# Two-layer hybrid decoder on one core: forms of the w_out product made earlier, one product keyed behind another, the norm's transposes without their key

## The chip, the core and the metric

The kernel runs on one NeuronCore of a Trainium2 chip. TensorE (PE) multiplies, VectorE (DVE) and ScalarE (ACT) do elementwise work and empty the PSUM banks, GpSimd (POOL) computes small powers, SyncE (SP) issues the DMAs. Each engine takes its own instructions in the order in which they stand; engines wait for one another by semaphores. The metric is the device time of one execution in microseconds (us): the median of three runs of the kernel before is 2274.98 us (2274.42 to 2275.09).

## The reference

Two decoder layers on 512 tokens of width 1024, all in fp32. Cut to what matters here:

```python
def hybrid_layer(x, ...):
    proj = rmsnorm(x, norm1_g) @ w_in
    y_ssd, y_mla, y_gdn = ...                 # three branches
    mixed = g_ssd * (y_ssd @ w_ssd_out) + g_mla * (y_mla @ w_mla_out) + g_gdn * (y_gdn @ w_gdn_out)
    h = x + mixed @ w_out
    f = jnp.square(jax.nn.relu(rmsnorm(h, norm2_g) @ w_up)) @ w_down
    return h + f
```

The change touches `mixed @ w_out` in both layers, the norm that follows it, and the end of the first layer's `@ w_down` with the next layer's first norm.

## The kernel before, in words

**Precision.** An fp32 operand is split into a high half (a rounded copy, made by ACT) and a low half (the difference, made by DVE). A product of two such operands is three matmuls: high by high, low by high, high by low (`mm3`, lines 196 to 200). Weights are split tile by tile into `whi` (line 170, ACT) and `wlo` (line 171, DVE); each has four buffers, so a cast for a new tile waits until PE has left the tile four places before it.

**Seven products.** `mixed @ w_out` (and `@ w_down`) is done by `seven` as a 2 x 2 block product with seven multiplications in place of eight. Tokens and the inner dimension are cut into halves on one side, the inner dimension and the columns on the other. On the feature side stand sums and differences of blocks, called forms: a11, a12, s1, s2, s4, s3, a22, named in the order in which w_out multiplies them. So a12 is the second product, s4 the fifth, s3 the sixth and a22 the seventh. One product has four weight tiles (k = 0 to 3) and two halves of rows (t = 0, 1), so 4 x 2 x 3 = 24 matmuls of 512 columns. It accumulates on a pair of PSUM banks: the pair x carries a11, s2, s3 and a22, the pair z carries s1 and s4, a12 has two banks of its own (`sm`). After each product that finishes a block of h, DVE adds the bank into h (line 1219), ACT then squares and sums h for the norm (line 289). a22 goes on accumulating on x after s3, so it can start on a bank only when line 1219 has read it.

**Forms.** In w_out a form has four pieces (d = 0 to 3, one per 128 features): `comb` (line 1299, DVE) makes the sum or difference, `put` writes its high half (line 1294, ACT) and low half (line 1295, DVE). Pieces 0 and 1 need features 0, 1, 4 and 5 of `mixed`, which are final before the last part of the third branch's projection; pieces 2 and 3 need features 6 and 7, which that last part gives. It runs in `mid`, between the first and the second product. The forms a12, s1, s2 and s4 lie in the tiles `xh`, `xl` of the normalized input, which PE reads for the last time in that same part (its gate product).

**Norm.** `norm_half` (lines 297 to 312) norms two blocks of 128 tokens: the two halves' sums of squares are added (line 293, DVE), scaled (276, DVE), raised to the power -1/2 (277, POOL), and h is multiplied by that into a tile `f` (303, DVE). PE then transposes both rows' tiles in 16 transposes (line 308), four to a bank, with three banks; ACT (272, `xh`) and DVE (273, `xl`) empty them with the norm's gain. The norm of the first two token blocks is issued ahead of a22, since their h is final after s4 in w_out.

**What sets the order.** A scheduler orders each engine's instructions from priorities and dependencies; it may place a later product's matmuls between those of an earlier one. `behind(key, ins)` adds an order-only edge: the instruction stands behind the matmul that `place(key, ...)` registered, here (stage, form, k, t). It moves places in the queue and adds no semaphore wait. `tc.high_priority()` raises what is issued in it.

Before, the transposes of the first two banks (`k < 4`) carry the key of a22's first weights on the first half, (a22, 0, 0), so they stand behind three of a22's matmuls. The sixth product has no key. The forms are made when their product is issued (`pre(n)`), all four pieces together.

Of the kernel before, what the change touches and what calls it, by code (L numbers as in the profile page):

```python
# [20 lines left out]
P = 128  # L21
S = 512
T = S // P
D = 1024
# [31 lines left out]
def hybrid_kernel(ctx, tc, a, out, depth=2, taps=None):  # L56
# [139 lines left out]
    def mm3(o, ah, al, bh, bl, start, stop, more=False):  # L196

        pe.matmul(o, ah, bh, start=start, stop=False, skip_group_check=more)  # L198
        pe.matmul(o, ah, bl, start=False, stop=False, skip_group_check=more)  # L199
        return pe.matmul(o, al, bh, start=False, stop=stop, skip_group_check=more)  # L200
# [96 lines left out]
    def norm_half(i, xs, ssq, gcol, pl, hs, ls, tag="xr", bufs=4, given=None, key=None):  # L297

        xr = given or []
        for t in (2 * i, 2 * i + 1)[len(xr) :]:  # L300
            rs = row_scale(ssq[t])
            xr.append(mk(pl, [P, D], F32, tag, bufs))
            dve.tensor_scalar(xr[-1], xs[t], rs, None, ALU.mult)
        for k in range(0, KD, 2):
            ps = sm_bank()
            for j in range(4):
                kk = k + j // 2
                x = pe.transpose(ps[:, j * P : (j + 1) * P], xr[j % 2][:, kk * P : (kk + 1) * P], ident)
                if key and k < 4:
                    behind(key, x)  # L310
            for j in range(2):
                split_gain(hs[k + j][:, HALVES[i]], ls[k + j][:, HALVES[i]], ps[:, j * 256 : (j + 1) * 256], gcol(k + j))
# [71 lines left out]
    for ly in range(depth):  # L384
# [810 lines left out]
        def seven(pl, ops, b, sq=None, before_last=None, fin=None, nf=4, pre=None, mid=None, prep=None, early=False, tag=None):  # L1195
# [29 lines left out]
            def mul(ps, n, w, k, t, start):  # L1225
                ah, al = (o[:, k % 2 * 256 + t * P : k % 2 * 256 + (t + 1) * P] for o in ops[n][k // 2])
                place((tag, n, k, t), mm3(ps[t], ah, al, *w[k], start and k == 0, k == 3, not start))
# [37 lines left out]
        with tc.tile_pool(name="wo", bufs=1, reuse_waits="tile") as wo:  # L1265
# [19 lines left out]
            def mid():  # L1285
# [4 lines left out]
                ops["a22"] = ck_pair()  # L1290

# [17 lines left out]
            def forms(n):  # L1309
# [3 lines left out]
                for d in range(4):  # L1313
                    with tc.high_priority() if d > 1 and n in ("a12", "s1") else nullcontext():
                        form(n, d)
# [20 lines left out]
            def n2(i, pl, *tag):  # L1336
                if not nf:
                    nf.extend(hilo_tags(lp, "x"))
                norm_half(i, hts, ssq, lambda k: col(g_n2 + k), pl, *nf, *tag, key=None if i else ((ly, "o"), "a22", 0, 0))
# [19 lines left out]
        with tc.tile_pool(name="ff", bufs=1, reuse_waits="tile") as fp:  # L1359
# [55 lines left out]
            def ends(qd):  # L1415
# [12 lines left out]
                def before_last():  # L1428
                    for t in range(2):
                        fin(t)  # L1430
                    if not last:
                        norm_half(0, hts, h_ssq, lambda k: params[0][:, 124 + k : 125 + k], fp, *nx, "f", 4, key=((ly, "d"), "a22", 0, 0))
# [51 lines left out]
```

## Time and profile before

| what | value |
|---|---|
| median of three runs | 2274.98 us (2274.42 to 2275.09) |
| the profiled execution | 2274.29 us, its span 2272.5 us |
| PE busy | 2252.4 us, 99% of the span, 11758 matmuls |
| weight loads on PE busy | 1867.6 us, 82% |
| DVE busy | 1649.5 us, 73%, 3315 instructions |
| ACT busy | 1186.1 us, 52%, 2444 instructions |
| POOL busy | 65.0 us, 3%, 84 instructions |
| granted TensorE clock, mean | 0.999 |
| DMA | 244.07 MB, mean 107 GB/s |

Times in a row of the timeline are microseconds from the span's start. A row gives start, duration, engine, line, operation, what is written and read (output, an arrow, inputs, without buffer numbers), and in brackets the engine's idle time before it with what ended it. Matmuls overlap: a 512-column matmul has a duration of 0.39 us, but the next starts about 0.23 us after it, so the pitch of the starts says how fast PE goes, and a start that comes later than the pitch is a hole. The ends of PE's instructions are modelled.

### The profile page before, as it was taken

To read this page: it belongs to the slowest core of one execution; us is meant where nothing else is said; L and a number is where in the kernel's file an instruction comes from. 1 tells how busy PE (TensorE), PEld (TensorE's weight loads), DVE (VectorE), ACT (ScalarE), POOL (GpSimd) and SP (SyncE) were. 2 spreads that over 40 slices of the span, in tenths; PEclk is the share of its full clock that TensorE was granted. 3 is DMA by queue.
4 is the path that set the end of the run, shared out by engine and by line. 5 is a ranking of instruction groups with operands and counts; after the bars stand their busy time and mean duration, and the time that the engine had idled before them with its cause. 6 is when DMAs were issued, how large, how long until landed. Compare 5 with 4: busy or idle time off the path is not lost.

```text
span 2272.5 us, 32127 instructions
## 1 busy us (share of the span) xinstructions
PE 2252.4 (99%) x11758; PEld 1867.6 (82%) x11758; DVE 1649.5 (73%) x3315; ACT 1186.1 (52%) x2444; POOL 65.0 (3%) x84
## 2 busy tenths in 40 slices
PE   9999999999999999999999999999999999999998
PEld 8888888888888888888888878888888887888886
DVE  7886567776766778767868865678657667778668
ACT  6666744333443555554656667443344435645545
POOL 1000000000000000000010000000001000000000
PEclk9999999999999999999999999999999999999999
DMA  4223633442225143233132246335422251433231
GB/s 143 81 75 110 190 108 119 137 134 75 84 65 176 56 149 111 93 110 103 52 99 81 71 121 195 104 110 148 121 84 75 66 189 34 167 112 102 84 111 47
DMA packets 220030, 244.07 MB, mean 107 GB/s; under 512 B 34256, under 2 KB 172384, under 8 KB 219872
## 3 DMA queue, kind: packets, MB, share of 16 engines
q1 hardware_dynamic: 219872, 242.02, 34.7%
q8 instruction: 92, 1.51, 0.3%
q14 instruction: 66, 0.54, 0.1%
HBM read 225.53 MB, written 11.74 MB: 104 GB/s over the span
## 4 chain that ended last, share of the span: by engine, by line
PE 95%; DVE 3%; DMA 1%; ACT 1%; issue 0%; POOL 0%; SPq 0%; DVEq 0%; POOLq 0%; ACTq 0%
PE acc L198 24%; PE acc L200 24%; PE acc L199 24%; PE sm L200 3%; PE sm L199 3%; PE sm L198 3%; PE sm L687 1%; PE sm L791 1%; DVE wlo L171 1%; PE yt L703 1%; PE sm L1073 1%; PE sm L802 1%; PE sm L1099 1%; PE yt L200 1%; PE yt L199 1%; PE yt L198 1%
## 5 line engine op out<-in xcount | busy, mean ns | idle before, releaser
L171 DVE TENSOR_TENSOR wlo<-wraw,whi 128x512 fp32r<-128x512 f32 (+1 forms) x536 | 365.4, 686 | 336.3 <-ACT whi L170 325.3
L170 ACT CAST whi<-wraw 128x512 fp32r<-128x512 f32 (+1 forms) x536 | 329.5, 618 | 524.1 <-PE acc L199 339.7
L198 PE MATMUL acc<-xh,whi 128*128 128x512 f32 (+1 forms) x1344 | 525.3, 391 | 0.0
L200 PE MATMUL acc<-xh,wlo 128*128 128x512 f32 (+1 forms) x1344 | 520.4, 388 | 0.0
L199 PE MATMUL acc<-xl,whi 128*128 128x512 f32 (+1 forms) x1344 | 519.2, 387 | 0.0
L200 PEld LDWEIGHTS acc<-xh,wlo 128*128 128x128 f32 x1344 | 252.5, 188 | 49.3
L198 PEld LDWEIGHTS acc<-xh,whi 128*128 128x128 f32 x1344 | 252.5, 188 | 48.4 <-ACT xh L272 0.4
L199 PEld LDWEIGHTS acc<-xl,whi 128*128 128x128 f32 x1344 | 252.7, 188 | 47.6 <-DVE xl L273 0.7
L170 ACT CAST whi<-wr 128x512 fp32r<-128x512 f32 x168 | 104.3, 621 | 107.9 <-PE acc L199 47.7
L198 PE MATMUL acc<-yh,whi 128*128 128x512 f32 x384 | 152.1, 400 | 0.0
L199 PE MATMUL acc<-yl,whi 128*128 128x512 f32 x384 | 150.3, 391 | 0.0
L200 PE MATMUL acc<-yh,wlo 128*128 128x512 f32 x384 | 149.8, 390 | 0.0
L171 DVE TENSOR_TENSOR wlo<-wr,whi 128x512 fp32r<-128x512 f32 x168 | 113.1, 685 | 35.6 <-ACT whi L170 34.7
L728 DVE SCALAR_TENSOR_TENSOR ckl<-acc,pc,ckl 128x511 f32<-128x511 f32 (+2 forms) x168 | 121.2, 743 | 19.2 <-ACT ckl L724 10.9
L198 PEld LDWEIGHTS acc<-yh,whi 128*128 128x128 f32 x384 | 71.5, 188 | 16.4 <-ACT yh L272 2.2
L200 PEld LDWEIGHTS acc<-yh,wlo 128*128 128x128 f32 x384 | 72.1, 188 | 15.1
L199 PEld LDWEIGHTS acc<-yl,whi 128*128 128x128 f32 x384 | 72.1, 188 | 14.2
L198 PE MATMUL acc<-whi,xh 128*128 128x512 f32 (+1 forms) x208 | 80.3, 386 | 1.2 <-DVE ckl L728 1.2
L199 PE MATMUL acc<-wlo,xh 128*128 128x512 f32 (+1 forms) x208 | 79.3, 381 | 0.0
L200 PE MATMUL acc<-whi,xl 128*128 128x512 f32 (+1 forms) x208 | 79.2, 382 | 0.0
L1219 DVE TENSOR_TENSOR h<-h,acc 128x512 f32<-128x512 f32 x120 | 76.9, 679 | 1.3 <-PE acc L200 1.3
L487 ACT ACTIVATE eE<-eE,cum 128x128 f32<-128x128 f32 x192 | 62.5, 390 | 27.9 <-DMA eE<-d_c 26.2
(468 smaller groups left out, 4497.8 us busy)
## 6 DMA issues: line engine op xcount, KB each, us to landing
wraw<-in_w_in_dram SPq DMA_DIRECT2D x144, 512.0 KB, 3.6
wraw<-in_w_up_dram SPq DMA_DIRECT2D x64, 512.0 KB, 3.5
wr<-in_w_down_dram SPq DMA_DIRECT2D x32, 1024.0 KB, 5.1
eE<-d_c SPq DMA_DIRECT2D x48, 256.0 KB, 4.1
wraw<-in_w_mla_out_dram SPq DMA_DIRECT2D x16, 512.0 KB, 3.4
eE<-d_e SPq DMA_DIRECT2D x32, 256.0 KB, 2.9
wraw<-in_w_ssd_out_dram SPq DMA_DIRECT2D x16, 512.0 KB, 3.3
wraw<-in_w_gdn_out_dram SPq DMA_DIRECT2D x16, 512.0 KB, 3.5
```

The source lines that it names most:

```text
L170: act.copy(hi, raw)
L171: dve.tensor_tensor(lo, raw, f32(hi), ALU.subtract)
L198: pe.matmul(o, ah, bh, start=start, stop=False, skip_group_check=more)
L199: pe.matmul(o, ah, bl, start=False, stop=False, skip_group_check=more)
L200: return pe.matmul(o, al, bh, start=False, stop=stop, skip_group_check=more)
L487: act.activation(o[:, i], o[:, i], AF.Relu, scale=-1.0, bias=cum[:, t, h0 + i : h0 + i + 1])
L687: pe.transpose(ps[:, n : n + P], pn[t][:, kb * P : (kb + 1) * P], ident)
L703: pe.matmul(o, v_h, th[:, c : c + w], start=kb == 0, stop=False)
L728: dve.scalar_tensor_tensor(acc[:, d:], ps[:, : S - d], taps_[3 - d], acc[:, d:], ALU.mult, ALU.add)
L791: x = pe.matmul(py[64 * i : 64 * i + 64, c * P : (c + 1) * P], xd[:, t, h * 64 : (h + 1) * 64], e2[h // 4][:, h % 4, :], start=True, stop= ...
L802: pe.matmul(po[:, c * P : (c + 1) * P], st[:, c * P : (c + 1) * P], ctl[:, tok], start=True, stop=True)
L1219: dve.tensor_tensor(hs_, hs_, ps[t], op)
```

## The change

1. In `mid`, behind the last part of the projection, pieces 0 and 1 of a12, s1, s2, s4 and a22 are made at once, in place of with their products; `forms` then makes pieces 2 and 3 only (a11 keeps all four).
2. `mm3` takes a key for its first matmul. In w_out, and in the stage of w_down that is followed by a layer, s3's first matmul on either half stands behind the last of s4.
3. The norm's transposes lose their key. In its place the row scales and the scaling into `f` of the first two token blocks are issued at high priority.

No matmul, transpose, DMA or elementwise operation is added or taken away: each engine has as many rows as before. SP's and POOL's orders don't change. Line numbers move (199 to 201, 200 to 202, 303 to 306, 308 to 311, 1219 to 1220).

```diff
-    def mm3(o, ah, al, bh, bl, start, stop, more=False):
+    def mm3(o, ah, al, bh, bl, start, stop, more=False, key=None):
 
-        pe.matmul(o, ah, bh, start=start, stop=False, skip_group_check=more)
+        x = pe.matmul(o, ah, bh, start=start, stop=False, skip_group_check=more)
+        if key:
+            behind(key, x)
...
         for t in (2 * i, 2 * i + 1)[len(xr) :]:
-            rs = row_scale(ssq[t])
-            xr.append(mk(pl, [P, D], F32, tag, bufs))
-            dve.tensor_scalar(xr[-1], xs[t], rs, None, ALU.mult)
+            with tc.high_priority() if first else nullcontext():
+                rs = row_scale(ssq[t])
+                xr.append(mk(pl, [P, D], F32, tag, bufs))
+                dve.tensor_scalar(xr[-1], xs[t], rs, None, ALU.mult)
...
-                x = pe.transpose(ps[:, j * P : (j + 1) * P], xr[j % 2][:, kk * P : (kk + 1) * P], ident)
-                if key and k < 4:
-                    behind(key, x)
+                pe.transpose(ps[:, j * P : (j + 1) * P], xr[j % 2][:, kk * P : (kk + 1) * P], ident)
...
-                place((tag, n, k, t), mm3(ps[t], ah, al, *w[k], start and k == 0, k == 3, not start))
+                key = (tag, "s4", 3, 1) if tag and early and n == "s3" and k == 0 else None
+                place((tag, n, k, t), mm3(ps[t], ah, al, *w[k], start and k == 0, k == 3, not start, key))
...
                 ops["a22"] = ck_pair()
+                for d in range(2):
+                    for n in ("a12", "s1", "s2", "s4", "a22"):
+                        form(n, d)
...
-                for d in range(4):
+                for d in range(0 if n == "a11" else 2, 4):
```

The two callers of `norm_half`, in `n2` and at the end of w_down, pass `first=not i` and `first=True` in place of the key.

**Order of PE, fifth and sixth product in the first layer's w_out.** acc_1589 and acc_1590 are the pair z, acc_1587 and acc_1588 the pair x; whi_1692 to whi_1698 are s4's weights, whi_1702 is s3's first; xh6 and xh7 hold s4's form. Before:

```order
L200 MATMUL acc_1590_7455<-whi_1692_7884,xl6_1645_7688 128x512
L198 MATMUL acc_1587_7452<-whi_1702_7931,s3h0_1583_7448 128x512
L198 MATMUL acc_1588_7453<-whi_1702_7931,s3h0_1583_7448 128x512
L198 MATMUL acc_1589_7454<-whi_1694_7894,xh6_1637_7680 128x512
L199 MATMUL acc_1589_7454<-wlo_1695_7895,xh6_1637_7680 128x512
```

Of the change:

```order
L202 MATMUL acc_1590_7455<-whi_1692_7888,xl6_1645_7688 128x512
L198 MATMUL acc_1589_7454<-whi_1694_7898,xh6_1637_7680 128x512
L201 MATMUL acc_1589_7454<-wlo_1695_7899,xh6_1637_7680 128x512
...
L202 MATMUL acc_1590_7455<-whi_1698_7918,xl7_1646_7689 128x512
L198 MATMUL acc_1587_7452<-whi_1702_7935,s3h0_1583_7448 128x512
```

s3's first two matmuls stood between s4's first and second weights; now they stand behind all of s4.

**Order of PE, s3, a22 and the transposes there.** f_1729 and f_1731 are the scaled rows of token blocks 0 and 1, ct_0 is the identity, whi_1736 and whi_1738 are a22's first and second weights. Before:

```order
L200 MATMUL acc_1588_7453<-whi_1708_7961,s3l1_1586_7451 128x512
L198 MATMUL acc_1587_7452<-whi_1736_8049,ckh0_1647_7690 128x512
L199 MATMUL acc_1587_7452<-wlo_1737_8050,ckh0_1647_7690 128x512
L200 MATMUL acc_1587_7452<-whi_1736_8049,ckl0_1649_7692 128x512
L308 MATMUL sm_1732_8005<-ct_0_75,f_1729_7997 128x128
L308 MATMUL sm_1732_8005<-ct_0_75,f_1731_8003 128x128
...
L198 MATMUL acc_1587_7452<-whi_1738_8053,ckh0_1647_7690 128x512
```

Of the change:

```order
L202 MATMUL acc_1588_7453<-whi_1708_7965,s3l1_1586_7451 128x512
L311 MATMUL sm_1732_8009<-ct_0_75,f_1729_8001 128x128
L311 MATMUL sm_1732_8009<-ct_0_75,f_1731_8007 128x128
...
L198 MATMUL acc_1587_7452<-whi_1736_8049,ckh0_1647_7690 128x512
L201 MATMUL acc_1587_7452<-wlo_1737_8050,ckh0_1647_7690 128x512
L202 MATMUL acc_1587_7452<-whi_1736_8049,ckl0_1649_7692 128x512
L198 MATMUL acc_1587_7452<-whi_1738_8053,ckh0_1647_7690 128x512
```

Twelve transposes (three banks) change places with a22's first three matmuls. The last four stay behind ten matmuls of a22. At the end of w_down the twelve move in the same way, and the last four move three matmuls back.

**Order of DVE, the norm's scaling in w_out.** h_1573 is h, wlo_1705 to wlo_1709 are low halves of s3's weights, wlo_1737 to wlo_1741 of a22's, nrs_1728 and nrs_1730 the row scales. Before:

```order
L1219 TENSOR_TENSOR h_1573_7426<-h_1573_7426,acc_1590_7455 128x512
L171 TENSOR_TENSOR wlo_1709_7962<-wr01_1575_7433,whi_1708_7961 128x512
L293 TENSOR_TENSOR nrs_1728_7993<-nss_1517_7123 128x1
L171 TENSOR_TENSOR wlo_1737_8050<-wr00_1663_7750,whi_1736_8049 128x512
...
L303 TENSOR_SCALAR f_1729_7997<-h_1573_7426,nrs_1728_7993 128x1024
L171 TENSOR_TENSOR wlo_1739_8054<-wr00_1663_7750,whi_1738_8053 128x512
L303 TENSOR_SCALAR f_1731_8003<-h_1573_7426,nrs_1730_7999 128x1024
L1219 TENSOR_TENSOR h_1573_7426<-h_1573_7426,acc_1587_7452 128x512
```

Of the change:

```order
L1220 TENSOR_TENSOR h_1573_7426<-h_1573_7426,acc_1590_7455 128x512
L171 TENSOR_TENSOR wlo_1709_7966<-wr01_1575_7433,whi_1708_7965 128x512
L295 TENSOR_TENSOR nrs_1728_7997<-nss_1517_7123 128x1
...
L306 TENSOR_SCALAR f_1729_8001<-h_1573_7426,nrs_1728_7997 128x1024
L171 TENSOR_TENSOR wlo_1737_8050<-wr00_1669_7778,whi_1736_8049 128x512
L171 TENSOR_TENSOR wlo_1739_8054<-wr00_1669_7778,whi_1738_8053 128x512
L306 TENSOR_SCALAR f_1731_8007<-h_1573_7426,nrs_1730_8003 128x1024
L171 TENSOR_TENSOR wlo_1741_8058<-wr00_1669_7778,whi_1740_8057 128x512
L1220 TENSOR_TENSOR h_1573_7426<-h_1573_7426,acc_1587_7452 128x512
```

The four small operations on nrs stand together and the first scaling directly behind them; a22's first low half moves behind it, and a third low half of a22 now stands ahead of the eviction of s3.

On ACT the same stage changes in two ways: the two squares that the scaling needs stand together ahead of a22's first cast (before, that cast stood between them), and one of the norm's gain copies (line 272) stands ahead of the two squares of s3's block, the rest behind them.

More of the change, by code (lines that the diff above doesn't have):

```diff
@@ L295, in row_scale, with norm_half @@
         return rs
-    def norm_half(i, xs, ssq, gcol, pl, hs, ls, tag="xr", bufs=4, given=None, key=None):
+    def norm_half(i, xs, ssq, gcol, pl, hs, ls, tag="xr", bufs=4, given=None, first=False):
         xr = given or []
         for t in (2 * i, 2 * i + 1)[len(xr) :]:
-            rs = row_scale(ssq[t])
-            xr.append(mk(pl, [P, D], F32, tag, bufs))
-            dve.tensor_scalar(xr[-1], xs[t], rs, None, ALU.mult)
+            with tc.high_priority() if first else nullcontext():
+                rs = row_scale(ssq[t])
+                xr.append(mk(pl, [P, D], F32, tag, bufs))
+                dve.tensor_scalar(xr[-1], xs[t], rs, None, ALU.mult)
         for k in range(0, KD, 2):
@@ L1338, in n2 @@
                     nf.extend(hilo_tags(lp, "x"))
-                norm_half(i, hts, ssq, lambda k: col(g_n2 + k), pl, *nf, *tag, key=None if i else ((ly, "o"), "a22", 0, 0))
+                norm_half(i, hts, ssq, lambda k: col(g_n2 + k), pl, *nf, *tag, first=not i)
             seven(wo, ops, b, ssq, lambda: n2(0, wo, "f", 2), nf=2, pre=forms, mid=mid, early=True, tag=(ly, "o"))
@@ L1431, in before_last @@
                     if not last:
-                        norm_half(0, hts, h_ssq, lambda k: params[0][:, 124 + k : 125 + k], fp, *nx, "f", 4, key=((ly, "d"), "a22", 0, 0))
+                        norm_half(0, hts, h_ssq, lambda k: params[0][:, 124 + k : 125 + k], fp, *nx, "f", 4, first=True)
                 return dict(sq=h_ssq, before_last=before_last, fin=fin, prep=prep, early=not last, tag=(ly, "d"))
```

## The prediction

> **What bounds the kernel now.** I read the page first, then who TensorE waits for, then the timeline of the stages that the edits touch.
>
> ```profile
> span 2272.5 us, 32127 instructions
> PE 2252.4 (99%) x11758; PEld 1867.6 (82%) x11758; DVE 1649.5 (73%) x3315; ACT 1186.1 (52%) x2444; POOL 65.0 (3%) x84
> ```
>
> TensorE (PE) is idle for 2272.5 - 2252.4 = 20.1 us of the whole span. The change adds or removes no matmul, so it can only win PE's waits at its three places: the two w_out products (one in each layer) and the end of the first layer's w_down. The waits by releaser, in total us, times, longest:
>
> ```profile
> PE acc L198 <- DVE h L1219: 3.5, 3, 1.2
> PE acc L198 <- ACT whi L170: 1.5, 2, 0.8
> ```
>
> Three waits for an eviction of h and two for a weight's high half are the two longest groups. Where they lie, on PE, in time (start, us, in brackets the idle time and its releaser):
>
> ```profile
> 774.29 0.39 PE L198 MATMUL acc<-whi,xh 128*128 128x512 f32 x1
> ...
> 786.53 0.40 PE L200 MATMUL acc<-whi,xl 128*128 128x512 f32 x1
> 787.69 0.73 PE L198 MATMUL acc<-whi,s3h 128*128 128x512 f32 x2 [0.76 <-ACT whi L170]
> ...
> 797.20 0.39 PE L200 MATMUL acc<-whi,s3l 128*128 128x512 f32 x1
> 798.77 0.47 PE L198 MATMUL acc<-whi,ckh 128*128 128x512 f32 x1 [1.18 <-DVE h L1219]
> ...
> 799.53 1.47 PE L308 MATMUL sm<-ct,f 128*128 128x128 f32 x12
> 800.76 0.48 PE L198 MATMUL acc<-whi,ckh 128*128 128x512 f32 x1
> ...
> 802.24 0.39 PE L198 MATMUL acc<-whi,ckh 128*128 128x512 f32 x1
> 802.58 0.63 PE L308 MATMUL sm<-ct,f 128*128 128x128 f32 x4
> ```
>
> This is layer 0: products s1, s2, s4, s3 from 774.29 to 797.20, then a22 with the norm's transposes in it. The second layer has the same two holes, so I count everything of this place twice:
>
> ```profile
> 1914.34 0.74 PE L198 MATMUL acc<-whi,s3h 128*128 128x512 f32 x2 [0.76 <-ACT whi L170]
> 1925.41 0.47 PE L198 MATMUL acc<-whi,ckh 128*128 128x512 f32 x1 [1.18 <-DVE h L1219]
> ```
>
> The pitch of one 512-column matmul comes from the product before, which has no hole:
>
> ```profile
> 769.76 0.39 PE L199 MATMUL sm<-wlo,xh 128*128 128x512 f32 x1
> ...
> 774.07 0.39 PE L200 MATMUL sm<-whi,xl 128*128 128x512 f32 x1
> ```
>
> 19 steps in 4.31 us, 0.2268 us each.
>
> **The sixth product behind the fifth, forms made ahead (term A, w_out only).** s1, s2, s4 and s3 are 4 x 24 = 96 matmuls. Without a hole, first start to last start is 95 x 0.2268 = 21.54 us; the rows say 797.20 - 774.29 = 22.91. So 1.37 us is lost, most of it ahead of 787.69. The cause on ScalarE (ACT):
>
> ```profile
> 787.02 0.62 ACT L170 CAST whi<-wr 128x512 fp32r<-128x512 f32 x1 [0.77 <-PE acc L200]
> 787.74 0.42 ACT L1294 ACTIVATE xh<-fc 128x256 fp32r<-128x256 f32 x1
> ```
>
> PE has s3's first two matmuls in its queue ahead of s4's second weights. Their weight cast can only start when PE has left s4's first weights (same buffer), 0.49 us after the start at 786.53, and the form that s4 needs next (787.74) stands behind that cast on ACT. PE waits for a thing that itself waited for PE. In the new order s4's 24 matmuls stand together, and s4's first two pieces of form were made long before. The key alone would leave PE waiting for that form; both edits are needed. I take all 1.37 off: s3's last matmul starts at 795.83.
>
> What the moved forms cost where they go: for s2 and s4, pieces 0 and 1, four combinations and four low halves on VectorE (DVE), four high halves on ACT.
>
> ```profile
> 753.16 0.69 DVE L171 TENSOR_TENSOR wlo<-wraw,whi 128x512 fp32r<-128x512 f32 x1 [0.50 <-ACT whi L170]
> 755.23 0.76 DVE L1295 SCALAR_TENSOR_TENSOR xl<-fc,xh 128x256 fp32r<-128x256 f32 x2 [1.37 <-ACT xh L1294]
> ...
> 758.60 0.69 DVE L171 TENSOR_TENSOR wlo<-wraw,whi 128x512 fp32r<-128x512 f32 x1 [1.86 <-ACT whi L170]
> ```
>
> Two of them take 0.76, with a pitch of 0.34, so 8 x 0.34 = 2.7 us go into 0.50 + 1.37 + 1.86 = 3.7 us of DVE idleness. On ACT the high halves wait until PE has read the old x tiles, as here, and weight casts queue behind:
>
> ```profile
> 754.77 0.73 ACT L1294 ACTIVATE xh<-fc 128x256 fp32r<-128x256 f32 x2 [1.64 <-PE sm L200]
> ...
> 760.67 0.62 ACT L170 CAST whi<-wr 128x512 fp32r<-128x512 f32 x1 [1.60 <-PE acc L199]
> 763.39 0.62 ACT L170 CAST whi<-wr 128x512 fp32r<-128x512 f32 x1 [2.10 <-PE acc L199]
> ```
>
> A cast comes late by 0.7 us at most, while the four weight buffers hold three more tiles of 2.7 us (763.39 - 760.67) each. So nothing on PE; without this cover it would cost at most 2 x 0.7. The 2.7 us leave the stretch 779.9 to 786.8, where DVE was busy for 6.85 of 6.90 us:
>
> ```profile
> 779.90:786.80 6.90, 6.90 (x30) 5.12 (x29) 6.85 (x15) 3.93 (x8) 0.00 (x0) 1.00 0.00 0
> ```
>
> **Transposes unkeyed, scaling first (term B).** a22 accumulates on the banks that s3 filled, so it must wait until DVE has added them into h. Before, the twelve transposes stood behind a22's first three matmuls and could not fill that wait; now they stand ahead of it. They need both scaled rows f, and the second of these, not s3, now ends last. Rows for the walk:
>
> ```profile
> 792.60 1.28 DVE L1219 TENSOR_TENSOR h<-h,acc 128x512 f32<-128x512 f32 x2
> ...
> 796.01 0.75 DVE L303 TENSOR_SCALAR f<-h,nrs 128x1024 f32<-128x1024 f32 x1 [0.42 <-POOL nrs L277]
> 796.68 0.68 DVE L171 TENSOR_TENSOR wlo<-wr,whi 128x512 fp32r<-128x512 f32 x1
> 797.28 0.75 DVE L303 TENSOR_SCALAR f<-h,nrs 128x1024 f32<-128x1024 f32 x1
> 797.94 1.28 DVE L1219 TENSOR_TENSOR h<-h,acc 128x512 f32<-128x512 f32 x2
> ```
>
> DVE starts its next operation 0.60 us after a wlo or h, 0.67 after an f. The new order on DVE is wlo, wlo, h, h, wlo, four small ones, f, wlo, wlo, f, wlo, h, h. Its second wlo waits for a cast that PE releases after s4's third weights: s4 starts at 774.29 + 48 x 0.2268 = 785.18, those weights' last matmul at 785.18 + 17 x 0.2268 = 789.03; + 0.49 + 0.62 for the cast is 790.14. Then h at 790.75 and 791.35, wlo at 791.95, the first small one at 792.55. From there to the first f the w_down stage, which has this order already, shows 1128.73 - 1127.66 = 1.07 (rows below): f at 793.62, wlo at 794.29 and 794.89, the second f at 795.49, done 796.24. From h's end to PE the rows show 797.94 + 0.68 = 798.62 to 798.77, 0.15 us. So the transposes start at 796.39, 0.33 after s3 (796.06), and take 800.76 - 799.53 = 1.23: 797.62. The first h eviction, behind f and a wlo, is over at 795.49 + 0.67 + 0.60 + 0.68 + 0.15 = 797.59, hidden by them. a22's first three matmuls take 0.76 (798.77 to 799.53), and its second weights start at 798.38. From s3's last matmul to there: 2.55 us, before 800.76 - 797.20 = 3.56. Gain 1.01.
>
> Some goes back. The last four transposes need a bank that DVE frees only after xl1, and between lie ACT's squares of the evicted h:
>
> ```profile
> 798.71 0.63 ACT L289 ACTIVATE fs<-h 128x512 f32<-128x512 f32 x1 [0.46 <-DVE h L1219]
> ...
> 800.17 2.44 ACT L272 ACTIVATE xh<-sm,pc 128x256 fp32r<-128x256 f32 x6
> ```
>
> In the new order ACT has one xh, the two squares, xh2, xh1. The first square follows the first h's end (797.44) by 0.09, the second comes 0.63 later, xh2 0.83 after that (800.17 less the second square's start, 798.71 + 0.63), xh1 0.40 later at 799.39. DVE's xl1 then ends near 800.4 and frees the bank for PE at some 800.55. PE comes there at 798.38 + 1.82 - 0.11 = 800.09 (1.82 is 802.58 - 800.76, 0.11 its own wait: 802.58 - 802.24 less one pitch). That wait is 0.46 where it was 0.11, so 0.35 go back: B = 1.01 - 0.35 = 0.66 at each w_out.
>
> At the w_down end DVE's order stays up to here; only the transposes move on PE.
>
> ```profile
> 1127.66 0.15 DVE L293 TENSOR_TENSOR nrs<-nss 128x1 f32<-128x1 f32 x1
> ...
> 1128.73 0.75 DVE L303 TENSOR_SCALAR f<-h,nrs 128x1024 f32<-128x1024 f32 x1 [0.43 <-POOL nrs L277]
> ...
> 1130.97 0.39 PE L200 MATMUL acc<-whi,mix 128*128 128x512 f32 x1
> ...
> 1131.04 0.74 DVE L303 TENSOR_SCALAR f<-h,nrs 128x1024 f32<-128x1024 f32 x1
> ...
> 1132.52 0.47 PE L198 MATMUL acc<-whi,yh 128*128 128x512 f32 x1 [1.17 <-DVE h L1219]
> ...
> 1134.52 0.48 PE L198 MATMUL acc<-whi,yh 128*128 128x512 f32 x1
> ```
>
> The second f ends at 1131.78; + 0.15 + 1.23 + 0.76 puts a22's second weights at 1133.92, before 1134.52: gain 0.60. The last four transposes now come three matmuls later, so their bank is free.
>
> **Sum.** 2 x (1.37 + 0.66) + 0.60 = 4.66, say 4.6 us. On the profiled execution: 2274.29 (span 2272.5 and 1.79 around it) becomes 2269.7, span 2267.9. The median of the runs is 2274.98, 0.69 above that execution, so I predict 2274.98 - 4.6 = 2270.4 us, 0.20% down. About 0.2%, 4.55 us, is what a measurement of this kernel can tell from no change, so my sum ends on that line.
>
> Bounds: the holes themselves hold 2 x (1.37 + 1.34) + 1.32 = 6.7 us (1.34 is 798.77 - 797.20 less one pitch, 1.32 is 1132.52 - 1130.97 less one); more can hardly come. Below, term B is open, since no row shows the transposes first: between 0 and 1.3 at each place.
>
> **The rivals.**
>
> *The power waits for DVE.* Two powers on POOL take 1.38 us, and the second lies beside the first f. In the new order f, wlo, wlo run back to back. Should the second power get no turn among them, it starts at 795.49, and the second f, with all behind it, is 0.6 later: 4.6 - 2 x 0.6 = 3.4, 2271.6. Against it:
>
> ```profile
> 795.42 1.38 POOL L277 TENSOR_TENSOR nrs<-nrs,nhalf 128x1 f32<-128x1 f32 x2 [101.70 <-DVE nrs L293]
> ```
>
> It ended at 796.80, 0.04 after f's end (796.76) and while the wlo of 796.68 ran; so f may hold it, a wlo hardly. With other small slips of the norm's chain I give it 0.14. (The Trainium skill, SBUF — State Buffer, section "SBUF: two separate sides", says that GpSimd and VectorE share a port pair as an exclusive lock, taken by a DVE operation in a 2-port mode or with two SBUF inputs when GpSimd reads SBUF. By that rule wlo, with two inputs, would hold the power as f does; this row agrees for f and speaks against it for wlo.)
>
> *Everything fits.* The squares and xh interleave better, the bank is free, f is in time: 2 x (1.37 + 1.2) + 0.9 = 6.0, 2269.0. The squares in ACT's order speak against it: 0.16.
>
> *The key only moves the wait.* s4 waits for its last two pieces of form instead, and A is gone: 2 x 0.66 + 0.60 = 1.9, 2273.1. DVE has 2.7 us less in that stretch, so 0.06.
>
> *Slower.* PE takes its queue in order, and with no key the transposes stand ahead of all 24 matmuls of a22. A late second f stops both. To be 4.55 us slower, the three B terms must come to -4.55 - 2.74 = -7.3, that is -2.4 each: from an f that is 3.1 us later than walked, five more DVE operations ahead of it. The order shows none, and DVE has 2.7 us less to do: 0.04.
>
> **How the numbers follow.** The forecast (gain 3.9 to 5.3) has 0.60, and half of it lies beyond 4.55. Faster: 0.31 + 0.16 = 0.47; within: 0.29 + 0.14 + 0.06 = 0.49; slower: 0.04. The range 2268.6 to 2272.4 takes in the first three cases and leaves out s4's wait, the slower case and the tails.
>
> **What would show it.** Right: no wait for whi at the start of s3 in w_out; transposes straight behind s3, with an idle time of some 0.3 us ahead of them; no 1.2 us wait for h; some 0.5 us ahead of the last four transposes; span near 2267.9. Wrong: a wait at s4's third weights (A has moved); transposes more than 1 us behind s3 (the norm's chain); weights late in the gate stage around 750 to 770.

## The result and the profile after

| | before | changed |
|---|---|---|
| median of ten runs | 2274.98 us | 2269.63 us |
| the profiled execution | 2274.29, span 2272.5 | 2269.02, span 2267.2 |
| PE busy | 2252.4 | 2251.3 |

The ratio of the runs is 0.9978 (the two medians alone give 0.9976), with a 95% interval of 0.997 to 0.9986. The interval lies below 1, so the changed kernel is faster. Its upper end is less than the 0.2% away from 1 that the prediction took as its line, so a gain above that line is not shown by the times. Predicted were 2270.4 us and a span of 2267.9. PE's idle time fell from 20.1 to 2267.2 - 2251.3 = 15.9 us. Page and waits of PE in the changed kernel (us in total, times, longest):

```profile
span 2267.2 us, 32128 instructions
...
PE 2251.3 (99%) x11758; PEld 1868.3 (82%) x11758; DVE 1649.1 (73%) x3315; ACT 1185.1 (52%) x2444; POOL 64.6 (3%) x84
```

```profile
PE acc L202 <- DVE wlo L171: 0.6, 1, 0.6
...
PE sm L311 <- DVE f L306: 0.4, 1, 0.4
...
PE sm L311 <- DVE xl L275: 0.2, 1, 0.2
```

The two longest waits of before, for h and whi, are gone from the list. Three small ones are new, and the largest is at a place of which the prediction said nothing. PE's timeline of the first layer's w_out in the changed kernel, with the same steps as shown of before (first matmul of s1, last of s3, transposes, a22's first and second weights, last four transposes, first matmul of w_up):

```profile
773.35 0.39 PE L198 MATMUL acc<-whi,xh 128*128 128x512 f32 x1
...
794.88 0.39 PE L202 MATMUL acc<-whi,s3l 128*128 128x512 f32 x1
795.11 1.57 PE L311 MATMUL sm<-ct,f 128*128 128x128 f32 x12
796.54 0.47 PE L198 MATMUL acc<-whi,ckh 128*128 128x512 f32 x1
...
797.31 0.39 PE L198 MATMUL acc<-whi,ckh 128*128 128x512 f32 x1
...
798.67 0.39 PE L198 MATMUL acc<-whi,ckh 128*128 128x512 f32 x1
799.23 0.63 PE L311 MATMUL sm<-ct,f 128*128 128x128 f32 x4 [0.17 <-DVE xl L275]
...
802.88 0.28 PE L198 MATMUL acc<-xh,whi 128*128 128x256 f32 x1
```

From s1 to s3's last matmul: 794.88 - 773.35 = 21.53 us, no hole. The transposes follow one pitch behind (0.23). From s3's last matmul to a22's second weights it is 2.43 us, where it was 3.56. The last four transposes come 0.56 behind a matmul whose pitch is 0.23. The hole of the gate stage, on PE and on DVE:

```profile
817.63 0.40 PE L201 MATMUL acc<-xl,whi 128*128 128x512 f32 x1
818.66 0.50 PE L202 MATMUL acc<-xh,wlo 128*128 128x512 f32 x1 [0.63 <-DVE wlo L171]
```

```profile
816.78 1.22 DVE L1181 TENSOR_TENSOR wp<-wr,wr 128x1024 f32<-128x1024 f32 x1 [2.18 <-DMA wr<-in_w_down_dram]
817.92 2.49 DVE L171 TENSOR_TENSOR wlo<-wraw,whi 128x512 fp32r<-128x512 f32 x4
```

DVE stood 2.18 us at a sum of w_down weights that waited for its transfer, while the wlo that PE needed stood behind it in DVE's queue. On PE the two starts lie 1.03 us apart where the pitch is 0.23, so 0.80 was lost there (the bracket counts from the modelled end of the matmul before). The casts of those tiles on ACT had begun a microsecond before the sum:

```profile
815.75 2.34 ACT L170 CAST whi<-wraw 128x512 fp32r<-128x512 f32 x4
```

**Stage by stage.** All kernels here issue the same number of matmuls on PE (11758), so the k-th start of one trace can be set against the k-th of another. The table gives what a run won against the profile of before between two marks (762.7 to 807.8 us, 807.8 to 823.2, 1122.8 to 1146.8, 1887.8 to 1933.6 on before's clock; medians of six starts around each mark). These differences are free of what happens elsewhere in the execution: by 762.7 us, ahead of PE's first reordered matmul, the thirteen runs already differ from before by -1.29 to +0.95 us (above 0 is ahead of it). The changed kernel's 0.95 does not come from the moved forms: DVE's order differs only from 743.65 us on, and by 300 us PE was already 0.94 ahead. A wait for `xr` in the first norm, 0.90 us in before (PE at 9.32) and 0.19 in the changed kernel (at 8.85), is 0.71 of it. One run of the kernel changed in the second layer only took 3202.27 us at a granted clock of 0.653; it is in that row's median, which is 2272.46 without it.

| run | first w_out | gate stage behind it | w_down's end | second w_out | time or median, us |
|---|---|---|---|---|---|
| changed | 2.43 | -0.99 | 0.85 | 2.37 | 2269.63 |
| changed, again | 2.43 | -1.06 | 0.84 | 2.34 | 2270.04 |
| forms alone | 1.27 | -0.59 | 0.00 | 1.22 | 2272.22 |
| key alone | -0.59 | -0.70 | 0.00 | -0.67 | 2276.45 (one run) |
| norm's part alone | 0.95 | -0.72 | 0.84 | 0.87 | 2271.55 |
| no key, no priority | 2.43 | -0.97 | 0.82 | 2.35 | 2269.23 (one run) |
| before, again | 0.03 | -0.01 | 0.03 | -0.03 | 2275.30 (one run) |
| sum held | 2.43 | -0.05 | 0.83 | 2.37 | 2268.84 |
| second f first | 2.24 | -0.71 | 0.84 | 2.21 | 2268.60 (one run) |
| last four later | 2.74 | -1.81 | 0.81 | 2.69 | 2270.39 (one run) |
| second layer only | 0.01 | 0.00 | 0.00 | 2.37 | 2272.51 |
| all three | 2.93 | -0.08 | 0.84 | 2.86 | 2268.69 |
| all three, again | 2.92 | -0.07 | 0.87 | 2.86 | 2268.44 |

For the changed kernel the four add up to 2.43 - 0.99 + 0.85 + 2.37 = 4.66 us. That is the prediction's sum to the second digit by luck, since the terms are others: 0.40 and 0.34 more at the two w_out, 0.25 more at w_down's end, and 0.99 lost where nothing was expected. The rest of the 5.27 us between the two profiled executions lies outside the change: 0.95 was there by 762.7 us, and 0.37 went back between w_down's end and the second w_out.

### The profile page after: what moved, and what is told of

Read it like the earlier page. It is cut to its first block, busy times and chain, and to the rows that moved or that the text cites. A ratio compares the mean times of both kernels' runs of the same rounds, so it can differ in the third digit from the quotient of the medians.

```text
span 2267.2 us, 32128 instructions
## 1 busy us (share of the span) xinstructions
PE 2251.3 (99%) x11758; PEld 1868.3 (82%) x11758; DVE 1649.1 (73%) x3315; ACT 1185.1 (52%) x2444; POOL 64.6 (3%) x84
## 4 chain that ended last, share of the span: by engine, by line
PE 95%; DVE 3%; DMA 1%; ACT 1%; POOL 0%; issue 0%; SPq 0%; DVEq 0%; POOLq 0%; ACTq 0%
PE acc L198 24%; PE acc L202 24%; PE acc L201 24%; PE sm L201 3%; PE sm L198 3%; PE sm L202 3%; PE sm L688 1%; PE sm L792 1%; DVE wlo L171 1%; PE yt L704 1%; PE sm L1074 1%; PE sm L1100 1%; PE sm L803 1%; PE yt L201 1%; PE yt L198 1%; PE yt L202 1%
## 5 line engine op out<-in xcount | busy, mean ns | idle before, releaser
L729 DVE SCALAR_TENSOR_TENSOR ckl<-acc,pc,ckl 128x511 f32<-128x511 f32 (+2 forms) x168 | 121.2, 743 | 19.2 <-ACT ckl L725 10.9
```

What stands on the lines that cost most here:

```text
L729: dve.scalar_tensor_tensor(acc[:, d:], ps[:, : S - d], taps_[3 - d], acc[:, d:], ALU.mult, ALU.add)
```

## The experiments

**Forms alone** (key on s3 off; the norm as before):

```diff
-                key = (tag, "s4", 3, 1) if tag and early and n == "s3" and k == 0 else None
+                key = None
```

> Only the early forms; no key on s3, the norm's transposes keyed and its scaling at plain priority, as before. Each engine's order is the same, row for row, as with forms and key together: with its form ready, s4 is taken whole ahead of s3 without the key. Theory (the early forms alone carry term A): from the start of s1 to the start of s3's last matmul 21.5 us in both layers (before 22.91), no whi wait at s3's start, and the norm still behind a22's first weights, so the 1.2 us wait for h stays; total gain near 2 x 1.37 = 2.7 us, profiled execution near 2271.6. In the first layer's gate stage of the feed-forward, the wait for wlo at 818 should be at most 0.3 us, since PE comes there 1.4 us early and not 3.3. Rival (both edits are needed, as the prediction says): 22.9 stays, no gain.

From s1 to s3's last matmul it took 21.53 us in both layers, and the wait for h stayed:

```profile
797.11 0.47 PE L198 MATMUL acc<-whi,ckh 128*128 128x512 f32 x1 [1.27 <-DVE h L1221]
```

The forms carry all of term A without the key. 1.27 and 1.22 us are won at w_out, less than term A's 1.37, since the wait for h grew by 0.1. The time, 2272.22 us, is 0.9991 of before (0.9982 to 1.0). In the gate stage the wait for wlo was 0.27 us, within the 0.3 that was expected, but by the starts on PE the stage lost 0.59.

**Key alone** (no early forms, the norm as before; against the changed kernel, its forms' lines are):

```diff
-                for d in range(2):
-                    for n in ("a12", "s1", "s2", "s4", "a22"):
-                        form(n, d)
...
-                for d in range(0 if n == "a11" else 2, 4):
+                for d in range(4):
```

> Only the key on s3; forms made with their products, norm as before. PE's order in w_out is that of the changed kernel up to the end of s3. Theory (the key only moves the wait): PE waits 1.2 to 1.5 us inside s4 for the second half of its form, s1's start to s3's last matmul stays at 22.5 to 23.1, execution within 0.5 us of 2275. Rival (the key carries term A): 21.5 and a gain of 2.7 us.

From s1's start to s3's last matmul it now took 23.35 and 23.37 us, more than the 22.5 to 23.1 that were expected. PE, inside s4, and ACT there:

```profile
788.61 0.50 PE L198 MATMUL acc<-whi,xh 128*128 128x512 f32 x1 [1.29 <-ACT xh L1297]
```

```profile
787.41 0.62 ACT L170 CAST whi<-wr 128x512 fp32r<-128x512 f32 x1 [0.77 <-PE acc L202]
788.14 0.42 ACT L1297 ACTIVATE xh<-fc 128x256 fp32r<-128x256 f32 x1
```

The key moved the wait from whi to the form, and made it longer: ACT still takes s3's cast ahead of the form, and now PE has nothing in between. 0.59 and 0.67 us were lost at w_out.

**The norm's part alone:** the forms' loops of the diff above taken out, and

```diff
-                key = (tag, "s4", 3, 1) if tag and early and n == "s3" and k == 0 else None
+                key = None
```

> Only the norm's part: transposes without key, scaling at high priority; no early forms, no key on s3. Theory (terms A and B are independent): s1's start to s3's last matmul stays at 22.9, the first transposes start 0.2 to 0.7 us behind s3's last matmul, s3's last to a22's first matmul 1.7 to 2.1, gain 0.6 to 1.0 at each w_out and 0.6 to 0.8 at w_down's end: 1.8 to 2.8 us in all. Rival (the norm is in time only because the early forms took work off DVE): the transposes more than 0.8 us behind s3 and a gain below 1.3 in all.

PE behind s3:

```profile
797.36 0.39 PE L202 MATMUL acc<-whi,s3l 128*128 128x512 f32 x1
797.59 0.27 PE L311 MATMUL sm<-ct,f 128*128 128x128 f32 x1
798.23 1.42 PE L311 MATMUL sm<-ct,f 128*128 128x128 f32 x11 [0.36 <-DVE f L306]
799.40 0.48 PE L198 MATMUL acc<-whi,ckh 128*128 128x512 f32 x1
```

The first transpose needs only the first f and starts at once; the second one waits for the second f. a22 starts 2.04 us behind s3's last matmul. It won 0.95 and 0.87 us at w_out and 0.84 at w_down's end; the time is 0.9988 of before (0.9979 to 0.9998). So each part works without the other: 1.27 + 0.95 = 2.22 against 2.43 together. The 0.2 more together goes with a second f that ends 0.32 us behind s3's last matmul there (below) and 0.81 here (798.17).

**No key, no priority:**

```diff
-            with tc.high_priority() if first else nullcontext():
+            with nullcontext():
...
-                key = (tag, "s4", 3, 1) if tag and early and n == "s3" and k == 0 else None
+                key = None
```

> The changed kernel without the key on s3 and without the high priority of the scaling: early forms and unkeyed transposes only. All five engines have the same order, row for row, as in the changed kernel. Theory (these two edits do nothing): every stage within 0.1 us of the changed kernel's (21.53, 0.23, 1.66, 29.54), time within 1.5 us of 2269.6. Rival (key or priority do something at run time): the whi wait of 0.76 or the h wait of 1.2 is back.

Four stretches of w_out are meant: from s1's first to s3's last matmul, from there to the first transpose and to a22's first matmul, and from s1's first matmul to w_up's. They are 21.53, 0.23, 1.66 and 29.55 us, within 0.03 of the changed kernel in both layers, and each engine has its rows in the changed kernel's order. Two of the four edits do nothing.

**Before, once more.** The forms, the key and the norm's part alone had each lost 0.59 to 0.72 us in the gate stage, even the key, with which PE comes there later than in before. So PE had not simply outrun the transfer. Perhaps the first profile of before was a lucky one:

> The kernel before, unchanged, profiled once more. Its first profile had no wait for wlo in the first layer's gate stage; its w_down weights had landed 9.0 us after the second of their four transfers was issued, against 10.5 to 10.9 us in the five profiles of other kernels so far. Theory (that landing varies by run, and the first profile of before was a lucky one): landing after some 10.5 us and a hole of 0.5 to 0.8 us at that place, execution 274.9 to 275.5 us above 2000. Rival (the hole belongs to the change): landing after 9.0 us and no hole, execution near 2274.3.

DVE there:

```profile
819.12 1.22 DVE L1180 TENSOR_TENSOR wp<-wr,wr 128x1024 f32<-128x1024 f32 x1
820.99 2.50 DVE L171 TENSOR_TENSOR wlo<-wraw,whi 128x512 fp32r<-128x512 f32 x4 [0.66 <-ACT whi L170]
```

There is no wait for the transfer and no hole on PE; the landing took 8.0 us. So the rival holds, as far as one repeat can show it. The execution took 2275.30 us, in the range of the first theory, but 1.29 of that was lost by 762.7 us, ahead of this place.

**The sum held** behind the wlo's of w_up's second column block:

```diff
+                    if c == 1:
+                        lo_c1 = lo_at[0]
+                    held[0] = lo_c1 if qd == 0 and c == 2 else None
                     after(c)
...
-                    dve.tensor_tensor(o[:, q], x[:, q], y[:, q], ALU.add)
+                    x_ = dve.tensor_tensor(o[:, q], x[:, q], y[:, q], ALU.add)
+                    if held[0]:
+                        after_product(x_.ins, held[0].ins)
```

(`lo_at` holds the last wlo that `split_half` issued; `after_product` adds an order-only edge.)

> The changed kernel, with the sum of w_down weight blocks (first quarter of w_down only, in both layers) ordered behind the wlo's of the second column block of w_up; nothing else moves on any engine. Theory (the sum waits for its transfer at the head of DVE's queue and holds back the wlo behind it): DVE makes those wlo from 816.4 on, the wait for wlo at 818 is gone, and 0.8 to 0.9 us are won in the first layer, nothing in the second: about 2268.8. Rival (the wlo are late for another reason, the casts on ACT): the wait stays at 0.6 us and the time at 2269.6.

DVE (line numbers are two higher here):

```profile
817.30 2.50 DVE L173 TENSOR_TENSOR wlo<-wraw,whi 128x512 fp32r<-128x512 f32 x4 [1.79 <-ACT whi L172]
```

The stage lost 0.05 in place of 0.99, though the transfer landed no sooner (10.9 us). So the wait hung on the sum's place in DVE's queue. By times alone this kernel can't be told from the changed one: its ratio to before is 0.9976 (0.9966 to 0.9985).

**The second f first:**

```diff
                     w.append(split_half(raw(k)))
+                    if n == "a22" and f_at[0]:
+                        after_product(lo_at[0].ins, f_at[0].ins)
```

(`f_at` holds the scaling into the second f.)

> The changed kernel, with DVE's second scaled row f ahead of all of a22's wlo (two or three operations later than f now). Prediction's reading (the second f ends last and sets when the transposes end and a22 starts, in w_out and at w_down's end): a22 starts 0.2 us earlier at each w_out (1.46 us behind s3's last matmul in place of 1.66) and 0.4 earlier at w_down's end. Rival (in w_out the eviction of h ends last, at 796.39, and the second f ends last only at w_down's end): twelve transposes in 1.23 us but a22's start at 1.6 to 1.7 in w_out, nothing gained there; 0.3 to 0.4 gained at w_down's end alone.

DVE and PE in the first w_out, and PE at w_down's end:

```profile
792.59 1.58 DVE L308 TENSOR_SCALAR f<-h,nrs 128x1024 f32<-128x1024 f32 x2 [0.38 <-POOL nrs L281]
...
795.89 1.28 DVE L1226 TENSOR_TENSOR h<-h,acc 128x512 f32<-128x512 f32 x2
```

```profile
795.12 1.47 PE L315 MATMUL sm<-ct,f 128*128 128x128 f32 x12
796.72 0.47 PE L200 MATMUL acc<-whi,ckh 128*128 128x512 f32 x1
...
1128.76 1.47 PE L315 MATMUL sm<-ct,f 128*128 128x128 f32 x12
1130.25 0.47 PE L200 MATMUL acc<-whi,yh 128*128 128x512 f32 x1
...
1134.06 0.63 PE L315 MATMUL sm<-ct,f 128*128 128x128 f32 x4
```

In w_out the transposes ran without a gap, and a22 came later, 0.83 us behind the start of h's eviction (795.89 to 796.72), as in the changed kernel (795.71 to 796.54, below). There the eviction ends last, not f. The second f now waited for the second power, so wlo and h moved back by 0.18, and w_out lost 0.19 and 0.16. At w_down's end f was last: a22 came 0.35 earlier. But PE then stood 0.29 us ahead of the last four transposes (0.51 behind a matmul whose pitch is 0.23), and the stage gave 0.84 as before. The gain there was nothing, where 0.3 to 0.4 was expected.

**The last four later:**

```diff
-                pe.transpose(ps[:, j * P : (j + 1) * P], xr[j % 2][:, kk * P : (kk + 1) * P], ident)
+                x = pe.transpose(ps[:, j * P : (j + 1) * P], xr[j % 2][:, kk * P : (kk + 1) * P], ident)
+                if key and k == 6:
+                    behind(key, x)
...
-                norm_half(i, hts, ssq, lambda k: col(g_n2 + k), pl, *nf, *tag, first=not i)
+                norm_half(i, hts, ssq, lambda k: col(g_n2 + k), pl, *nf, *tag, first=not i, key=None if i else ((ly, "o"), "a22", 0, 1))
```

> The changed kernel, with the last four transposes of w_out's norm behind a22's first weights on the second half, five matmuls later. The order also puts both halves of the w_down weight sum ahead of the wlo's at 818, in place of one. Theory: the bank is free when PE gets there, so the 0.33 us ahead of the last four transposes is gone (before them one pitch, 0.23) and a22's end comes 0.3 earlier at each w_out; and the doubled sum makes the wait for wlo in the first layer longer by one sum, 1.1 us, to some 1.8 us. Rival on the first: another bank wait stays ahead of them. Rival on the second (that wait doesn't hang on the sum): it stays at 0.6.

The bank was free: 2.74 and 2.69 us at w_out, 0.3 more than the changed kernel. The gate stage on DVE and PE:

```profile
818.18 2.36 DVE L1183 TENSOR_TENSOR wp<-wr,wr 128x1024 f32<-128x1024 f32 x2 [2.08 <-DMA wr<-in_w_down_dram]
```

```profile
821.20 0.50 PE L202 MATMUL acc<-xh,wlo 128*128 128x512 f32 x1 [1.46 <-DVE wlo L171]
```

Two sums stand ahead of the wlo in place of one, and the loss grew from 0.99 to 1.81. The second sum holds DVE for 2.36 - 1.22 = 1.14 us and cost 0.82.

**The second layer only.** The same lines with `ly` in their conditions, the norm keyed as before where `ly` is 0 and at w_down's end:

```diff
-                for d in range(2):
+                for d in range(2 if ly else 0):
...
-                for d in range(0 if n == "a11" else 2, 4):
+                for d in range(0 if n == "a11" or not ly else 2, 4):
```

> The whole change in the second layer's w_out alone; up to there each engine's order is row for row that of before, the first layer's w_out and w_down end included. Theory one (the slow landing of the w_down weights in the first layer comes with something in the schedule of that layer's w_out): landing 8 to 9 us after the second of the four transfers is issued, as in the two profiles of before, no wait for wlo at 818, and the gain is that of one w_out, 2.4 us. Theory two (it is a property of the whole program, whatever stands near that place): landing after 10.5 to 10.9 us, a wait of 0.3 to 0.6 us there, and a gain of 1.5 to 2.1 us. On the change itself: the second layer's w_out at 21.53, 0.23, 1.66 and 29.55 us, whatever the first layer did.

It won 2.37 us in the second w_out and lost nothing in the first layer's gate stage, where the landing came after 7.94 us. The time is 0.999 of before (0.9981 to 0.9999), 2.40 us less by the medians. Theory two fails. Of theory one it is open what in the schedule would do it.

**All three additions together,** and in w_out a22's second to fourth wlo behind the first eviction of h:

```diff
+                        after_product(lo_at[0].ins, (h_at if mid and k else f_at)[0].ins)
```

(`h_at` holds the first eviction of s3.)

> The changed kernel with the w_down weight sum behind the wlo's of w_up's second column block, the last four transposes of w_out's norm behind a22's first weights on the second half, the second f ahead of a22's wlo (both places), and in w_out a22's second to fourth wlo behind the first eviction of h. Theory (what ends last in w_out is the eviction of h, at w_down's end the second f, then the bank): 0.9 us in the first layer's gate stage, 2 x 0.3 at the last four transposes, 2 x 0.1 to 0.2 at a22's start (1.46 to 1.55 us behind s3's last matmul, now 1.66), 0.35 at w_down's end: 2.1 us below the changed kernel, near 2267.5. Rival (one of them shifts to a wlo that comes late for a22's second or third weights): 0.2 to 0.4 us lost again in each w_out, near 2268.2.

PE behind s3:

```profile
796.59 0.39 PE L204 MATMUL acc<-whi,s3l 128*128 128x512 f32 x1
796.82 1.47 PE L315 MATMUL sm<-ct,f 128*128 128x128 f32 x12
798.04 0.48 PE L200 MATMUL acc<-whi,ckh 128*128 128x512 f32 x1
```

Now the transposes set a22's start (1.46 us behind s3), with no wait up to w_up. It won 2.93 and 2.86 us at the two w_out, lost 0.08 in the gate stage, and won nothing more at w_down's end, where 0.35 was expected. By stages that is 6.55 us against 4.66, 1.9 more than the change. The median, 2268.69 us, is above the 2267.5 that were expected; its ratio to before is 0.9973 (0.9963 to 0.9983).

**The changed kernel and all three again,** on one chip:

> The changed kernel, unchanged, profiled and timed once more beside the kernel with all three additions. So far the w_down weights of the first layer landed 7.9 to 8.9 us after the issue of the second transfer in four profiles (before twice, the change in the second layer alone, all three additions) and 10.5 to 10.9 us in eight (the changed kernel and six others among them). Theory one (each program has its own landing): 10.5 to 10.9 again, wait for wlo 0.6 us. Theory two (it varies from run to run): as likely fast as not here or in the next run; if it is fast, DVE's sum starts without delay and the wait is gone. Time near 2269.5; ratio to before near 0.9977.

> The kernel with all three additions, once more, on the same chip as the changed kernel. Theory one: landing after 8.0 us again. Theory two: fast or slow, without effect on the time here, since the sum no longer stands ahead of the wlo's. In both: stages 21.53, 0.23, 1.46 and 29.06 us at each w_out; median 0.9 to 2.0 us below that of the changed kernel: 2 x 0.49 from w_out and 0 to 0.9 from the gate stage, with 0.35 won and 0.30 lost again at w_down's end.

They took 2270.04 us (0.9978, 0.9969 to 0.9987) and 2268.44 us (0.9971, 0.996 to 0.9982): 1.6 us apart by the medians (2.0 by the stages), but the intervals overlap. The landing took 10.9 us for the changed kernel and 8.1 for the other, each near its first profile. That is what theory one says; with the repeat of before there are three pairs of profiles for it, and none against it.

## Why the prediction was right, point by point

In short: the two causes that the prediction named, and their places, are as it said. It held one edit for needed that isn't, made term B too small at all three places, and left out a loss of the same size in the gate stage. That these two errors cancel is luck.

**Term A: the size right, its cause half wrong.** 22.91 became 21.53 us, predicted 21.54. "Both edits are needed" fails. The forms alone bring it. With its form ready s4 is taken whole ahead of s3 without the key, and leaving out the key moved no row on any engine. Of the key alone the prediction said that it "would leave PE waiting for that form": so it did, for 1.29 us.

**The moved forms cost nothing on PE:** held. From 735 to 770 us, where they now stand, PE's lead over before stays at 0.95 us in the changed kernel and at 0.38 with the forms alone.

**Term B: 1.05 and 1.00 instead of 0.66** (the stage's 2.43 and 2.37 less term A's 1.38 and 1.37). The walk on DVE in the changed kernel, with POOL's powers:

```profile
792.58 0.75 DVE L306 TENSOR_SCALAR f<-h,nrs 128x1024 f32<-128x1024 f32 x1 [0.38 <-POOL nrs L279]
793.25 1.29 DVE L171 TENSOR_TENSOR wlo<-wr,whi 128x512 fp32r<-128x512 f32 x2
794.45 0.75 DVE L306 TENSOR_SCALAR f<-h,nrs 128x1024 f32<-128x1024 f32 x1
...
795.71 1.28 DVE L1220 TENSOR_TENSOR h<-h,acc 128x512 f32<-128x512 f32 x2
```

```profile
791.99 1.38 POOL L279 TENSOR_TENSOR nrs<-nrs,nhalf 128x1 f32<-128x1 f32 x2 [99.22 <-DVE nrs L278]
```

The second f ended at 795.20, 0.32 behind s3's last start; predicted 0.41. "The transposes start ... 0.33 after s3" missed that the first transpose reads only the first f: it started at once, one pitch behind s3 (0.23), and most of the f wait lay beside it. That "the first h eviction ... is ... hidden by them" was a tie in the walk (797.59 against 797.62) and came out the other way: the eviction ended last, as the f-first experiment shows. The front part, from s3's last matmul to a22's second weights, measured 3.56 - 2.43 = 1.13 for 1.01. The 0.35 to be given back was too large: the wait ahead of the last four transposes went from 0.11 to 0.33, which is 0.22. PE's first matmul of w_up, in before:

```profile
806.27 0.28 PE L198 MATMUL acc<-xh,whi 128*128 128x256 f32 x1
```

From a22's second weights to there it was 806.27 - 800.76 = 5.51, and is 802.88 - 797.31 = 5.57. So only 0.06 went back: the 0.22 at the transposes, less 0.12 on the way to them (1.48 before, 1.36 now) and 0.04 behind them (3.69 and 3.65). Of the 0.12, 0.08 is the first matmul behind a row of transposes, which in both traces takes 0.31 us to the next start in place of 0.23: in before it was that of a22's second weights, now it is that of its first. 1.13 - 0.06 is 1.07, and by the stage 1.05.

**w_down's end: 0.85 instead of 0.60.** The first transpose is missed here too. PE there, in the changed kernel:

```profile
1128.55 0.39 PE L202 MATMUL acc<-whi,mix 128*128 128x512 f32 x1
1128.78 0.27 PE L311 MATMUL sm<-ct,f 128*128 128x128 f32 x1
1129.42 1.42 PE L311 MATMUL sm<-ct,f 128*128 128x128 f32 x11 [0.37 <-DVE f L306]
...
1131.38 0.40 PE L198 MATMUL acc<-whi,yh 128*128 128x512 f32 x1
```

One transpose is done before the second f ends, and the others follow at a pitch of 0.11. a22's second weights came 2.83 us behind s3's last matmul, in place of 3.55 (1134.52 - 1130.97): 0.72. The rest of the 0.85 lies mostly in the matmuls that follow an idle stretch or a row of transposes, which take some 0.09 more to the next start (0.31 to 0.32 in both traces): two of them now, three before.

**"Scaling first" does nothing.** Without the priority no engine's order changes, so term B came from the transposes' missing key.

**What the sum left out: 0.99 in the gate stage.** The prediction followed the queues up to the transposes, not to the next instruction behind them that waits for a transfer. In before the sum stood there too, and cost nothing:

```profile
818.19 1.22 DVE L1180 TENSOR_TENSOR wp<-wr,wr 128x1024 f32<-128x1024 f32 x1 [0.26 <-DMA wr<-in_w_down_dram]
819.72 2.50 DVE L171 TENSOR_TENSOR wlo<-wraw,whi 128x512 fp32r<-128x512 f32 x4 [0.31 <-ACT whi L170]
```

SP's issue of the transfers, in before and in the changed kernel:

```profile
807.33 0.57 SPq L1186 DMA_DIRECT2D wr<-in_w_down_dram  x1
```

```profile
804.01 1.32 SPq L1187 DMA_DIRECT2D wr<-in_w_down_dram  x1
...
805.98 4.85 SPq L1187 DMA_DIRECT2D wr<-in_w_down_dram  x3
```

The issue moved with PE: 1.06 us behind w_up's first matmul in before (807.33 - 806.27), 1.13 now. What changed is the landing of the second transfer, 10.7 us after its issue (805.98) in place of 8.9 (from 809.18). With 8.9 it would have landed at 814.9, the sum would have been done near 816.1 (it holds DVE for 1.14, 816.78 to 817.92), ahead of the first cast's end (816.37, at 0.62 us for a cast), and by this estimate there would be no hole. No run changed the landing alone, but the profiles go with it: each of the eight with a landing of 10.5 us or more and the sum in its old place lost 0.59 to 1.81, and each of the three with 7.9 to 8.9 and the sum there lost nothing. That the sum's place carries the wait is shown by experiment: with the sum held back the loss was 0.05 at the same slow landing, and a second sum made it 0.82 larger. The forecast sum came out because the missed loss of 0.99 and the undersized gains (0.40 + 0.34 + 0.25) are equal, which nothing in the prediction foresaw.

**The rivals.** "The power waits for DVE" falls: the second power ended at 791.99 + 1.38 = 793.37, with the first f (ended 793.33), and over a microsecond ahead of the second f. (The Trainium skill, SBUF — State Buffer, section "SBUF: two separate sides", has a DVE operation with two SBUF inputs lock out a GpSimd that reads SBUF, and has the one that starts first keep the lock. The rows don't settle that here, POOL's times being rough. The second power ended 0.12 into a wlo. One that began 0.09 ahead of a wlo, at 802.79 in the changed kernel, took 0.55 us, and the wlo its usual 0.69. But one that began 0.12 into a wlo, at 1138.93 in before, took 0.81.) "The key only moves the wait" is what the key does alone, not in the change. "Everything fits" came nearest in w_out, at 2.43 for 2.57. "Slower" did not come, since f was in time.

## What to carry to other kernels

An instruction that waits for a transfer at the head of an in-order queue makes its landing time everybody's: follow a walk past the edited stage to the next such instruction, and order it behind what the bound engine needs. When several edits are made together, compare the order with each one left out: here two of four moved no row. And where a wait goes, ask which two or three things end within 0.1 us of each other behind it, since making one of them faster wins nothing.

## What the runs showed that was not expected

The first layer's w_down weights landed after 7.9 to 8.9 us or after 10.5 to 10.9 us, and in the programs profiled twice it went by program, not by run. The time is from issue to landing of the second transfer of the four, the only one whose landing the profile tells; in before and in the changed kernel:

```profile
wr<-in_w_down_dram SPq DMA_DIRECT2D x4, 1024.0 KB, 8.9
```

```profile
wr<-in_w_down_dram SPq DMA_DIRECT2D x4, 1024.0 KB, 10.7
```

Three programs were profiled twice: before 8.9 and 8.0, changed 10.7 and 10.9, all three additions 8.0 and 8.1. The second layer only had 7.9; the other seven 10.5 to 10.9. GB/s in slices of 0.4 us, from 1.3 us ahead of the first issue, in before and in the changed kernel:

```profile
GB/s 0 41 0 0 3 118 253 351 394 325 384 369 404 343 358 384 361 353 335 364 392 397 410 399 399 410 405 410 410 410 410 410 410 410 410 410 410 410 374 266
```

```profile
GB/s 0 0 41 0 23 115 241 330 364 195 110 187 284 328 353 338 307 361 343 305 348 358 364 392 404 389 410 407 405 410 404 410 410 410 410 399 410 410 410 410
```

The changed kernel's rate dips to 110 GB/s between 2.3 and 3.5 us behind the first issue, and before's doesn't. But the dip is not what the slow landing needs: in the changed kernel's second profile the rate stays at 284 GB/s or more from 2 us behind the first issue on, and the landing took 10.9 us all the same. SP's order is the same in all, and the key alone, which moves five rows in each w_out, has the slow landing, while the change in the second layer alone has the fast one. The kernel with all three additions, whose first layer is changed most, has the fast one too. What sets it was not found.
